# A written order from the output projection's last group to the MLP's third pair, with its norm by token halves

## The chip, the cores and the metric

The kernel runs on one core of one Trainium2 chip. The metric is device time in microseconds (us) of one execution, lower is better. Three runs of the kernel before took 2401.02, 2407.87 and 2409.24 us; their median, 2407.87, is the time before.

The core has five instruction streams that run beside each other and meet only at semaphores: PE (TensorE, matmuls; its weight loads are listed as PEld), DVE (VectorE), ACT (ScalarE), POOL (GpSimd) and SP (SyncE, which here only issues DMA transfers). Each stream works strictly in the order in which its instructions stand.

## The reference

One layer over 512 latent tokens of width 2048, with 256 context tokens as a prefix. All values are float32. The lines that matter here:

```python
mod_x = (silu(c) @ w_ada + b_ada)            # six rows of 2048: sh1, s1, g1, sh2, s2, g2
h  = rmsnorm(x, norm1_w) * (1 + s1) + sh1
q_da, k_da, v_da, q_mla, k_mla, v_mla = mixer_inputs(h, ...)   # projections of h, of the context too
o  = concat(differential attention, latent attention)          # 512 x 2048
x  = x + g1 * (o @ w_o)                                         # output projection
h2 = rmsnorm(x, norm2_w) * (1 + s2) + sh2                       # mean over the 2048 features of a token
g, u = split(h2 @ w_up)                                         # 2 x 5632
x  = x + g2 * ((silu(conv3(g)) * u) @ w_down)                   # conv3: over three neighbouring tokens
```

A final norm over `x` gives the output. `w_ada` is 2048 by 12288, so the modulation alone reads 96 MB.

## The kernel before

**Layout and precision.** Activations stand with features on the 128 partitions and the 512 tokens along the free axis, so a 2048-wide activation is 16 tiles of 128x512. Each float32 operand of a product is split into a high part (a rounded copy, made by ACT, `wh` for weights) and a low part (the remainder, made by DVE, `wl`), and a product is three matmuls: high·high, high·low, low·high (`mm3`, L107 to L109). Tiles are named after the buffers that they come from: `wr` raw weights of 128x1024, `a2k`, `q2k` and `b2k` activation tiles, `ada` a modulation row's weights, `xr` a tile of the residual `x`, `b` and `s` accumulators in PSUM.

**Weight blocks.** A block is 512 KB. SP issues its load into one of three raw buffers (`wraw`, L89), ACT makes the high part, DVE the low part, in one of three buffers each (`wblock`; L80 and L81 in the automatic order, L210 and L213 in the early written one, L1346 and L1352 in the late one).

**Modulation rows.** `gemv` (L171, L174) computes 128 of the 12288 modulation values: one 1 MB load into one of two `ada` buffers, then one multiply-and-sum on DVE over 128x2048. 64 of them are strewn over the program by `next_gemv`, one at a time, where the author of the order put them. In the early stages they are loaded by POOL's queue, in the output projection by SP's.

**The stages around the change.** First, the value stage: eight blocks of `w_v` go into six accumulators (`v0`), DVE and ACT write them away as high and low parts (`put_value`, the function `lay`), and the blocks of the next features follow. This region's order is written out: `step` puts a block's matmuls, then the high and low part of the block two further, then a list of small tasks; these tasks are the numbers of `plan` (L750) and the arguments at L790 and L791. In it nothing reorders.

Second, the output projection: the 16 output tiles are made in four groups of four; a group is eight blocks of `w_o`, 192 matmuls, 512 tokens wide. DVE then adds each accumulator to the residual (L1119), POOL's queue writes the result to `x1_d`, and ACT squares it; POOL adds the squares up over groups 0 to 2. The last four squares go straight into PE. `token_norm` (L1085) sums over features by a matmul with ones, L1093, ten passes at full width, and `rstd` (L162 to L167) makes the inverse root on ACT and DVE with one refinement step.

Third, the first pair of the MLP (`first_pair`): eight blocks of `w_up`, 384 products of 128x128 by 128x256 (the tokens in two halves), into four accumulators. Before a block, `normed` (L1155 to L1160) makes its two normed tiles, with high and low parts of each token half; `sums` (L1173 to L1181) makes from tiles j and j+8 the four sums of token halves and features that a Strassen-like scheme uses as moving operands in all later pairs. Between them stand the four "u" blocks (a third, classical, pair). Pair 3 is the first of that scheme (`run`, kind "p", L1376 and L1378). Its weights come through two rings of three raw buffers on SP's queue: ring a (`wr`) and ring b (`rb`, `Ring`, L1259).

From the output projection to the end of the first pair an automatic scheduler sets the order: it lists instructions per engine by its own estimate of when each can run. From the u blocks on the order is written out again (`tc.manual_schedule`): each engine's instructions stand as the Python code emits them.

## Time and profile before

| What | Before |
|---|---|
| median of 3 runs | 2407.87 us |
| profiled execution, its own time | 2408.41 us |
| its span, first to last instruction | 2406.6 us |
| PE busy | 2337.9 us (97%) |
| DVE busy | 1774.7 us (74%) |
| ACT busy | 1100.5 us (46%) |
| mean granted clock of TensorE | 0.992 |
| first matmul of output groups 0 to 3 | 835, 878.26, 921.80, 965.30 us |
| last group's end, first matmul of pair 3 | 1008.80, 1099.4 us |

The page gives for each engine its busy time, and for each group of instructions (by source line, engine, operation and tile) the number, busy time, mean duration and the idle time before them with what ended it. "L174 DVE ... ada<-ada" is read as: line 174 of the kernel, VectorE, writes `ada` from `ada`. A value in brackets with an arrow, such as "[2.40 <-DMA ada<-in_ada]", says how long the engine had waited before that instruction, and for what. "Granted clock" is the share of TensorE's full clock that it was given.

### The profile page before, as it was taken

To read this page: it belongs to the slowest core of one execution; us is meant where nothing else is said; L and a number is where in the kernel's file an instruction comes from. 1 tells how busy PE (TensorE), PEld (TensorE's weight loads), DVE (VectorE), ACT (ScalarE), POOL (GpSimd) and SP (SyncE) were. 2 spreads that over 40 slices of the span, in tenths; PEclk is the share of its full clock that TensorE was granted. 3 is DMA by queue.
4 is the path that set the end of the run, shared out by engine and by line. 5 is a ranking of instruction groups with operands and counts; after the bars stand their busy time and mean duration, and the time that the engine had idled before them with its cause. 6 is when DMAs were issued, how large, how long until landed. Compare 5 with 4: busy or idle time off the path is not lost.

```text
span 2406.6 us, 32350 instructions
## 1 busy us (share of the span) xinstructions
PE 2337.9 (97%) x12444; PEld 1967.4 (82%) x12444; DVE 1774.7 (74%) x2303; ACT 1100.5 (46%) x1660; POOL 271.2 (11%) x324
## 2 busy tenths in 40 slices
PE   8999999999999999999999999999999999999997
PEld 5787888777677788798888888888888888888887
DVE  5996787698878877597585757575767676766767
ACT  5322332455555622354454545454545454544553
POOL 0001001121100011200101010101010101111113
PEclk9999999999999999999999999999999999999999
DMA  9767877844311189514646454555554545455572
GB/s 381 280 224 273 307 286 291 246 138 121 119 42 49 61 317 346 186 59 135 143 130 144 128 143 136 140 140 140 134 147 126 150 120 157 123 157 123 140 213 78
DMA packets 141514, 407.45 MB, mean 169 GB/s; under 512 B 14880, under 2 KB 31792, under 8 KB 130736
## 3 DMA queue, kind: packets, MB, share of 16 engines
q1 hardware_dynamic: 107296, 298.42, 37.0%
q0 software_dynamic: 32912, 105.93, 18.2%
q8 instruction: 97, 1.59, 0.3%
q10 hardware_dynamic: 1152, 1.05, 0.1%
q14 instruction: 57, 0.47, 0.1%
HBM read 335.86 MB, written 69.48 MB: 168 GB/s over the span
## 4 chain that ended last, share of the span: by engine, by line
PE 69%; issue 14%; DVE 8%; ACT 3%; DMA 3%; POOL 2%; SPq 0%; POOLq 0%; DVEq 0%; ACTq 0%
PE y L1376 11%; PE b L107 7%; PE b L108 7%; PE b L109 7%; PE z L1376 6%; PE y L1378 5%; PE s L882 3%; PE z L1378 3%; PE x L1376 2%; PE s L108 2%; PE s L107 2%; PE s L109 2%; PE pt L894 1%; PE f L107 1%; PE x L1378 1%
## 5 line engine op out<-in xcount | busy, mean ns | idle before, releaser
L1397 POOL DMA_DIRECT2D x_d<-xs x160 | 140.6, 1018 | 1167.3 <-ACT xs L1396 1148.4
L107 PE MATMUL b<-ah,wh 128*128 128x512 f32 (+1 forms) x672 | 259.1, 386 | 0.0
L108 PE MATMUL b<-al,wh 128*128 128x512 f32 (+1 forms) x672 | 259.0, 385 | 0.0
L109 PE MATMUL b<-ah,wl 128*128 128x512 f32 (+1 forms) x672 | 258.0, 384 | 0.0
L1352 DVE TENSOR_TENSOR wl<-wr,wh 128x1024 fp32r<-128x1024 f32 x126 | 153.8, 1221 | 130.3 <-ACT wh L1346 130.2
L1352 DVE TENSOR_TENSOR wl<-rb,wh 128x1024 fp32r<-128x1024 f32 x124 | 151.1, 1220 | 127.5 <-ACT wh L1346 127.5
L1346 ACT CAST wh<-wr 128x1024 fp32r<-128x1024 f32 x126 | 132.3, 1050 | 206.9 <-PE b L108 100.5
L1346 ACT CAST wh<-rb 128x1024 fp32r<-128x1024 f32 x124 | 130.2, 1051 | 187.8 <-PE b L108 116.1
L1352 DVE TENSOR_TENSOR wl<-ws,wh 128x1024 fp32r<-128x1024 f32 x123 | 150.1, 1220 | 89.3 <-ACT wh L1346 89.3
L174 DVE CUSTOM_DVE_ANT_0 ada<-ada,cb,smt 128x2048 f32<-128x2048 f32 x64 | 153.5, 2401 | 58.5 <-DMA ada<-in_ada 58.5
L1346 ACT CAST wh<-ws 128x1024 fp32r<-128x1024 f32 x123 | 128.2, 1042 | 139.3 <-PE b L108 45.5
L109 PEld LDWEIGHTS b<-ah,wl 128*128 128x128 f32 x672 | 126.3, 188 | 25.6
L107 PEld LDWEIGHTS b<-ah,wh 128*128 128x128 f32 x672 | 126.6, 188 | 22.8
L108 PEld LDWEIGHTS b<-al,wh 128*128 128x128 f32 x672 | 126.6, 188 | 22.0
L107 PE MATMUL b<-a2k,wh 128*128 128x512 f32 (+1 forms) x352 | 135.2, 386 | 6.7 <-ACT a2k L1159 5.1
L109 PE MATMUL b<-a2k,wl 128*128 128x512 f32 (+1 forms) x352 | 133.2, 378 | 3.3 <-DVE wl L213 3.3
L80 ACT CAST wh<-wr 128x1024 fp32r<-128x1024 f32 (+2 forms) x64 | 64.2, 1003 | 135.3 <-PE s L108 44.3
L81 DVE TENSOR_TENSOR wl<-wr,wh 128x1024 fp32r<-128x1024 f32 (+2 forms) x64 | 77.8, 1215 | 42.5 <-ACT wh L80 42.3
L1376 PE MATMUL y<-b2k,wh 128*128 128x512 f32 x410 | 106.9, 391 | 0.0
L884 DVE TENSOR_REDUCE m<-s 128x1 f32<-128x768 f32 x96 | 90.1, 948 | 20.8 <-PE s L882 20.4
L1396 ACT ACTIVATE xs<-b,modx 128x512 f32<-128x512 f32 x160 | 101.1, 681 | 2.0 <-DMA x_d<-xs 1.6
L210 ACT CAST wh<-wr 128x1024 fp32r<-128x1024 f32 x38 | 39.9, 1050 | 126.7 <-DMA wr<-in_w_f 40.3
(536 smaller groups left out, 6095.7 us busy)
## 6 DMA issues: line engine op xcount, KB each, us to landing
rb<-in_w_up SPq DMA_DIRECT2D x123, 512.0 KB, 4.4
ada<-in_ada POOLq DMA_DIRECT2D x54, 1024.0 KB, 6.2
wr<-in_w_dn SPq DMA_DIRECT2D x84, 512.0 KB, 3.8
x_d<-xs POOLq DMA_DIRECT2D x160, 256.0 KB, 6.1
wr<-in_w_up SPq DMA_DIRECT2D x53, 512.0 KB, 4.2
ada<-in_ada SPq DMA_DIRECT2D x26, 1024.0 KB, 6.6
wr<-in_w_f SPq DMA_DIRECT2D x34, 512.0 KB, 6.2
adak<-in_ada_k SPq DMA_DIRECT2D x64, 256.0 KB, 5.4
```

The source lines that it names most:

```text
L81: ve.tensor_tensor(dst_l, src, dst_h.bitcast(F32), op=ALU.subtract)
L107: pe.matmul(out, st[0], mv[0], start=start, stop=False, **kw)
L108: pe.matmul(out, st[0], mv[1], start=False, stop=False, **kw)
L109: pe.matmul(out, st[1], mv[0], start=False, stop=stop, **kw)
L174: ve.tensor_tensor_reduce(out=junk, in0=w, in1=vec, op0=ALU.mult, op1=ALU.add, scale=1.0, scalar=col("b_ada", j), accum_out=dst[:, j:j + 1])
L884: ve.tensor_reduce(out=m, in_=s[:, :TT], axis=AX.X, op=ALU.max, negate=True)
L1346: sc.copy(hi, raw)
L1352: ve.tensor_tensor(lo, raw, hi.bitcast(F32), op=ALU.subtract)
L1376: pe.matmul(o, w[j][0], hs[j], start=start and j == 0, stop=False, skip_group_check=True)
L1378: pe.matmul(o[:, h0], w[j][1], hs[j][:, h0], start=False, stop=j == 7, skip_group_check=True)
L1396: sc.mul(x, po, modx[:, 80 + dt:81 + dt])
L1397: gp.dma_start(x1_d[dt], x, accum_op=ALU.add)
```

## The change

The change has two parts. One is small and early: in the value stage, the writing away of values 0 and 5 (`lay`) is put one step earlier, into the last value block's tasks, in the place of a modulation row, and the two steps behind it have three modulation rows where they had four, so that this place holds two rows fewer. Those two are made in the output projection instead, where every group now has a row ahead of its eighth block too.

The other part takes the stretch from the output projection's last group to the u blocks out of the automatic scheduler's hands and writes its order out for all five engines. In that order:

- weight blocks come by `load8`, `cast8`, `low8`: the load of block i+3 is issued by SP when DVE has made the low part of block i, and stands in SP's order directly behind it; a modulation row (`next_gemv`) stands behind each low part of the last output group;
- output blocks 6 and 7 run first for the first token half, then for the second; the sums of squares, the matmuls with ones, the root and the normed tiles are made by token halves, and the first two `w_up` blocks run by halves as well (`unit`);
- the normed tiles are held in tiles of the pools that the Strassen operands use (`tp`, `q2k(0)`), the sums are cut in two (`first` makes differences and high parts, `second` the low parts) and dealt out from a list by `some`;
- ring a's first loads follow from the same list of blocks; ring b's first loads are issued behind the third u block, where before both rings were filled at once;
- the convolution and activation of the first two feature tiles stand ahead of the u blocks, in PSUM tiles of the earlier pools.

The number of products, of modulation rows and of bytes loaded stays the same.

The diff, cut to its core (of the written region the added lines only):

```diff
+        def lay(t, own=False):
+            return lambda: put_value(0, v0, t, [rtmp(F32R), rtmp(F32R)] if own else None)
...
-                [gemvs(1), gemvs(1)], [gemvs(1), bias_out, gemvs(1)])
+                [gemvs(1), gemvs(1)], [gemvs(1), bias_out, lay(0), lay(5)])
...
-        step(block(1, 0), lay(0), lay(5), gemvs(1), lay(1, True), gemvs(1))
-        step(block(1, 1), lay(2), lay(3), gemvs(1), lay(4, True), gemvs(1))
+        step(block(1, 0), lay(1, True), gemvs(1), lay(2), gemvs(1))
+        step(block(1, 1), lay(3), gemvs(1), lay(4, True))
...
+    aq_ = [tc.alloc_tile_pool(name=f"aq{i}", bufs=8, side="right", reuse_waits="tile") for i in range(2)]
+
+    def q2k(i, dt=F32):
+        return aq_[i].tile([P, 512], dt, tag="q2k", name=nm("q2k"))
...
+    def square_tile():
+        return wx.tile([P, T], F32, tag="sq", name=nm("sq"), bufs=2)
+
+    def residual(dt):
+        xr = wx.tile([P, T], F32, tag="xr", name=nm("xr"), bufs=6)
+        nc.sync.dma_start(xr, x_t[dt])
+        return xr
+
+    def evict(dt, out, xr, c=slice(0, T)):
+        ve.scalar_tensor_tensor(out=x1[dt][:, c], in0=out[:, c], scalar=modx[:, 32 + dt:33 + dt], in1=xr[:, c],
+                                op0=ALU.mult, op1=ALU.add)
+
+    def out_block(outs, kb, w, c=slice(0, T), skip=True):
+        order = [(j, i) for j in range(2) for i in range(4)]
+        for j, i in sorted(order, key=lambda t: t[1]) if kb == 7 else order:
+            kt, o = kb * 2 + j, j * 512 + i * P
+            mm3(outs[i][:, c], [t[:, o:o + P] for t in w], [t[:, c] for t in osp[kt]], kt == 0, kt == 15, skip)
+
+    h0, h1 = slice(0, HT), slice(HT, T)
+    UP = [kb for j in range(4) for kb in (j, j + 4)]
+    src8 = [w_o[3, kb] for kb in range(8)] + [w_up0[kb] for kb in UP] + [w_up[0, 0, i] for i in range(2)]
+    raw8, hl8 = {}, {}
+
+    def load8(i):
+        if i < len(src8):
+            raw8[i] = wraw(src8[i])
+
+    def cast8(i):
+        hl8[i] = [wp.tile([P, 1024], F32R, tag=g, name=nm(g), bufs=3) for g in ("wh", "wl")]
+        sc.copy(hl8[i][0], raw8[i])
+
+    def low8(i):
+        ve.tensor_tensor(hl8[i][1], raw8.pop(i), hl8[i][0].bitcast(F32), op=ALU.subtract)
+        load8(i + 3)
+
+    x1, ss = [], wx.tile([P, T], F32, name="ss")
+    for g in range(3):
...
-            if kb != 7 if g else kb > 2:
+            if g or kb > 2:
                 next_gemv(wo, 1)
-            wh, wl = wblock(w_o[g, kb])
-            order = [(j, i) for j in range(2) for i in range(4)]
-            for j, i in sorted(order, key=lambda t: t[1]) if kb == 7 else order:
-                kt, o = kb * 2 + j, j * 512 + i * P
-                mm3(outs[i], (wh[:, o:o + P], wl[:, o:o + P]), osp[kt], kt == 0, kt == 15)
+            out_block(outs, kb, wblock(w_o[g, kb]), skip=False)
+        if g == 2:
+            for i in range(2):
+                hl8[i] = wblock(src8[i])
...
-        h = hf[kt] = hp.tile([P, T], F32, tag="h", name=nm("h"), bufs=5)
-        ve.scalar_tensor_tensor(out=h, in0=x1[kt], scalar=a2[:, kt:kt + 1], in1=r, op0=ALU.mult, op1=ALU.mult)
-        hx[kt] = (a2k(F32R), q2k(F32R) if kt >= 8 else hp.tile([P, T], F32R, tag="h12", name=nm("h12"), bufs=8))
...
+    def norm_in(kt, cs):
+        if ht[kt] is None:
+            ht[kt] = tp2k() if kt >= 8 else q2k(0)
+            hx[kt] = a2k(F32R), q2k(1, F32R) if kt >= 8 else hp.tile([P, T], F32R, tag="h12", name=nm("h12"), bufs=8)
+        c = slice(cs[0].start, cs[-1].stop)
+        ve.scalar_tensor_tensor(out=hview(kt, c), in0=x1[kt][:, c], scalar=a2[:, kt:kt + 1], in1=r[:, c],
+                                op0=ALU.mult, op1=ALU.mult)
+        for c in cs:
+            sc.activation(hx[kt][c is h1][:, h0], hview(kt, c), AF.Identity, bias=modx[:, 48 + kt:49 + kt])
+
+    def norm_low(kt, cs):
+        for c in cs:
+            hh, hl = half(hx[kt][c is h1])
+            ve.scalar_tensor_tensor(out=hl, in0=hview(kt, c), scalar=modx[:, 48 + kt:49 + kt], in1=hh.bitcast(F32),
+                                    op0=ALU.add, op1=ALU.subtract)
+
+    def normed(kts, *cs):
+        for kt in kts:
+            norm_in(kt, cs)
+        for kt in kts:
+            norm_low(kt, cs)
+
+    def scratch():
+        return hp.tile([P, T], F32, tag="d", name=nm("d"), bufs=2)
...
+        def first():
...
+            t1[j], t3[j], t2[j], t4[j] = q2k(0, F32R), tp2k(F32R), b2k(F32R), b2k(F32R)
+            for t, d in zip((t1, t2, t3, t4), ds):
+                sc.copy(half(t[j])[0], d)
...
+        def second():
+            for t, d in zip((t1, t2, t3, t4), ds):
+                hh, hl = half(t[j])
+                ve.tensor_tensor(hl, d, hh.bitcast(F32), op=ALU.subtract)
...
+    with tc.manual_schedule(engines=every):
+        for i in range(2, 5):
+            load8(i)
+        outs = [b_tile() for _ in range(4)]
+        xrs = []
+        for i in range(6):
+            out_block(outs, i, hl8.pop(i))
+            cast8(i + 2)
+            low8(i + 2)
+            next_gemv(wo, 2 if i == 2 else 1)
+            if i == 3:
+                xrs = [residual(12 + k) for k in range(4)]
+        wo.release()
+        hp = tc.alloc_tile_pool(name="hp", bufs=1, side="right", reuse_waits="tile")
+        r = hp.tile([P, T], F32, name="nr")
+        hp.tile([P, T], F32R, tag="h12", name=nm("h12"), bufs=8)
+        x1 += [b2k() for _ in range(4)]
+        for kb in (6, 7):
+            out_block(outs, kb, hl8[kb], h0)
+        s0, s1 = s_tile(), s_tile()
+        po = s0[:, :512]
+        fo = [s0[:, 512:], s1[:, :512], s1[:, 512:]]
+        sq = {}
+
+        def squares_of(c):
+            sq[c.start] = [t[:, k * HT:(k + 1) * HT] for t in (square_tile(), square_tile()) for k in range(2)]
+            for i in range(4):
+                evict(12 + i, outs[i], xrs[i], c)
+                sc.square(sq[c.start][i], x1[12 + i][:, c])
+
+        def ones_of(c):
+            qs = [ss[:, c]] + sq[c.start]
+            for q in qs:
+                pe.matmul(po[:, c], ones32, q, start=q is qs[0] and c is h0, stop=q is qs[-1], skip_group_check=True)
+
+        def root_of(c):
+            rstd(r[:, c], po[:, c], D, *half(scratch()))
+
+        def unit(n_, cs):
+            w = hl8[8 + n_]
             for j in range(2):
+                kt = UP[n_] * 2 + j
                 for i in range(4):
                     o = j * 512 + i * P
+                    classical(fo[i], kt, [t[:, o:o + P] for t in w], n_ == 0 and j == 0, n_ == 7 and j == 1, cs)
+
+        def pair(n_):
+            return [UP[n_] * 2 + j for j in range(2)]
+
+        cast8(8)
+        low8(8)
+        squares_of(h0)
+        out_block(outs, 6, hl8[6], h1)
+        ones_of(h0)
+        out_block(outs, 7, hl8[7], h1)
+        root_of(h0)
+        normed(pair(0), h0)
+        squares_of(h1)
+        for i in range(4):
+            gp.dma_start(x1_d[12 + i], x1[12 + i])
+        fo.append(b_tile())
+        unit(0, (h0,))
+        ones_of(h1)
+        cast8(9)
+        low8(9)
+        normed(pair(1), h0)
+        unit(1, (h0,))
+        cast8(10)
+        low8(10)
+        root_of(h1)
+        normed(pair(0), h1)
+        unit(0, (h1,))
+        normed(pair(1), h1)
+        cast8(11)
+        low8(11)
+        unit(1, (h1,))
+        normed(pair(2), h0, h1)
+        wx.release()
+        ff = tc.alloc_tile_pool(name="ff", bufs=1, reuse_waits="tile")
+        for n_ in range(2, 8):
+            unit(n_, (h0, h1))
+            cast8(10 + n_)
+            if n_ < 7:
+                normed(pair(n_ + 1), h0, h1)
+            low8(10 + n_)
+            some((0, 1, 2, 1, 2, 3)[n_ - 2])
...
-            items_a.append((job, w_up[0, job[1] // 2, job[1] % 2], 1))
+            if job[1] > 1:
+                items_a.append((job, w_up[0, job[1] // 2, job[1] % 2], 1))
...
-        ra, rb = Ring(wrp, "wr", 3, items_a), Ring(mm, "rb", 3, items_b)
+        ra = Ring(wrp, "wr", 3, items_a)
+        ra.pump()
...
-        cast(0)
-        low(0)
-        cast(1)
-        low(1)
+        for i in range(2):
+            ready[i] = *hl8.pop(16 + i), None, None
+        cast(2)
+        low(2)
+        for i in range(2):
+            t = convolve(i, fo[2 * i])
+            if i:
+                some(1)
+            acts[i] = multiply(silu(t), fo[2 * i + 1])
+            some(1 - i)
+            finish(t, acts[i])
+        ps_b.release()
+        ps_s.release()
...
+            if i == 2:
+                hp.release()
+                mm = tc.alloc_tile_pool(name="mm", bufs=1, side="right", reuse_waits="tile")
+                rb = Ring(mm, "rb", 3, items_b)
+                rb.pump()
...
-            cast(i + 2)
             if i:
+                cast(i + 2)
+            if i > 2:
                 act_after(i - 1)
                 vec_after(i - 1)
-            low(i + 2)
+            if i:
+                low(i + 2)
+            if i < 4:
+                some((2, 1, 0, 2)[i])
```

SP's order in the last output group, before from that group's fourth `w_o` block on, with the change from its sixth (`ada` a modulation row's load, `wr` a weight block's, the buffer numbers run on through the program). Before:

```order
L171 DMA ada_8700<-in_ada 128x2048
L89 DMA wr_8670<-in_w_o 128x1024
L171 DMA ada_8733<-in_ada 128x2048
L1117 DMA xr_8556<-in_x_t 128x512
L89 DMA wr_8703<-in_w_o 128x1024
L171 DMA ada_8766<-in_ada 128x2048
L89 DMA wr_8736<-in_w_o 128x1024
L89 DMA wr_8769<-in_w_o 128x1024
```

With the change:

```order
L89 DMA wr_8640<-in_w_o 128x1024
L171 DMA ada_8642<-in_ada 128x2048
L89 DMA wr_8673<-in_w_o 128x1024
L171 DMA ada_8675<-in_ada 128x2048
L89 DMA wr_8706<-in_w_o 128x1024
L171 DMA ada_8708<-in_ada 128x2048
L171 DMA ada_8711<-in_ada 128x2048
L89 DMA wr_8742<-in_w_up 128x1024
L171 DMA ada_8744<-in_ada 128x2048
```

Before, the loads of rows stood ahead of those of the weight blocks and the last of them ahead of the group's sixth block; now each row's load stands behind a weight block's load, down to those of `w_up`.

DVE's order at the same place (`wl` a low part, the two "ISA" rows of L174 one modulation row). Before, from the first low part of the group on:

```order
L81 TENSOR_TENSOR wl_8574<-wr_8571,wh_8573 128x1024
L174 ISA ada_8667,modx<-ada_8667,cb_7618,smt 128x2048
L174 ISA modx 128x1
L81 TENSOR_TENSOR wl_8607<-wr_8604,wh_8606 128x1024
L1119 SCALAR_TENSOR_TENSOR b2k_8534<-s_8269,modx,xr_8532 128x512
```

With the change, from its third low part on:

```order
L1114 TENSOR_TENSOR wl_8637<-wr_8602,wh_8636 128x1024
L174 ISA ada_8642,modx<-ada_8642,cb_7618,smt 128x2048
L174 ISA modx 128x1
L1114 TENSOR_TENSOR wl_8670<-wr_8604,wh_8669 128x1024
L174 ISA ada_8675,modx<-ada_8675,cb_7618,smt 128x2048
L1114 TENSOR_TENSOR wl_8703<-wr_8606,wh_8702 128x1024
L174 ISA ada_8708,modx<-ada_8708,cb_7618,smt 128x2048
L174 ISA ada_8711,modx<-ada_8711,cb_7618,smt 128x2048
L1114 TENSOR_TENSOR wl_8739<-wr_8640,wh_8738 128x1024
```

`wl_8670` stands behind the row whose load is `ada_8642`; SP's load `wr_8673` goes into the raw buffer that `wl_8670` reads, and the next row's load, `ada_8675`, stands behind it.

DVE's order behind the value stage (`beta` the copies at L735, `kl` and `rt` low parts of values). Before:

```order
L735 COPY beta<-b_1433 128x4
L174 ISA ada_2027,modx<-ada_2027,cb,smt 128x2048
L174 ISA modx 128x1
L81 TENSOR_TENSOR kl_2084<-b_1562,kh_2083 128x512
L213 TENSOR_TENSOR wl_2081<-wr_1959,wh_2080 128x1024
L81 TENSOR_TENSOR kl_2093<-b_1563,kh_2092 128x512
```

With the change:

```order
L735 COPY beta<-b_1433 128x4
L81 TENSOR_TENSOR kl_2028<-b_1562,kh_2027 128x512
L81 TENSOR_TENSOR kl_2034<-b_1563,kh_2033 128x512
L81 TENSOR_TENSOR rt_2093<-s_1560,rt_2092 128x512
L213 TENSOR_TENSOR wl_2090<-wr_1959,wh_2089 128x1024
L174 ISA ada_2101,modx<-ada_2101,cb,smt 128x2048
```

The row behind the copies is gone, and the two values that were written away behind and around the next low part stand ahead of it.

138 lines of the change are left out of this document (44 added, 94 removed).

## The prediction

> **What bounds the kernel now.** First the page's busy table, then the windows of the stretch that the change rewrites, from the last output group's first matmul (965.30) to the third MLP pair's first (1099.4).
>
> ```profile
> PE 2337.9 (97%) x12444; PEld 1967.4 (82%) x12444; DVE 1774.7 (74%) x2303; ACT 1100.5 (46%) x1660; POOL 271.2 (11%) x324
> ```
>
> ```profile
> 965.30:1008.80 43.50, 43.50 (x193) 36.05 (x192) 23.09 (x20) 10.71 (x13) 12.24 (x11) 1.00 0.58 203
> 1008.80:1019.25 10.45, 4.75 (x11) 1.63 (x10) 5.97 (x9) 5.11 (x9) 0.99 (x2) 0.96 0.45 172
> 1019.25:1086.00 66.75, 66.37 (x528) 66.14 (x528) 60.19 (x127) 38.00 (x78) 0.00 (x0) 0.95 0.20 66
> 1086.00:1099.40 13.40, 9.12 (x51) 8.64 (x51) 5.86 (x5) 3.07 (x4) 0.00 (x0) 0.75 0.51 184
> ```
>
> Columns are the stretch, its length, busy PE, PEld, DVE, ACT and POOL, the granted clock, the DMA share and GB/s. PE sets the pace and is full in the last output group; it idles 5.7 us around the norm and 4.3 us before pair 3, where the clock is 0.75 as well. The waits of PE name the two holes:
>
> ```profile
> PE b L107 <- ACT a2k L1159: 5.1, 1, 5.1
> PE z L107 <- ACT wh L1346: 3.6, 1, 3.6
> ```
>
> The first is the norm's chain, the second a w_up block whose load stood on SP behind three rb loads. With the slow clocks behind them the stretch, 134.1 us long, holds some 16 us that a better order could save. In the last output group DVE is half idle (23.09 of 43.50): all seven modulation rows (gemv, L174) of it are done at 979.9, because their loads ran ahead.
>
> **The first hunk (lay).** In the first value stage two modulation rows leave, and DVE reaches the splits sooner. One PE wait hangs on this:
>
> ```profile
> 257.99 2.35 DVE L174 CUSTOM_DVE_ANT_0 ada<-ada,cb,smt 128x2048 f32<-128x2048 f32 x1 [2.40 <-DMA ada<-in_ada]
> 260.27 1.22 DVE L213 TENSOR_TENSOR wl<-wr,wh 128x1024 fp32r<-128x1024 f32 x1
> 272.41 1.22 DVE L213 TENSOR_TENSOR wl<-wr,wh 128x1024 fp32r<-128x1024 f32 x1
> ```
>
> ```profile
> 273.69 0.50 PE L109 MATMUL b<-a2k,wl 128*128 128x512 f32 x1 [3.30 <-DVE wl L213]
> ```
>
> ```profile
> 270.00:274.00 4.00, 0.70 (x3) 0.30 (x2) 4.00 (x5) 1.16 (x2) 0.53 (x1) 1.00 0.59 131
> 274.00:280.00 6.00, 6.00 (x28) 5.13 (x26) 5.96 (x11) 0.67 (x2) 0.53 (x1) 0.72 0.87 355
> ```
>
> The split that PE wants at 270.4 ends at 273.6 since DVE waited for two modulation loads before 260. Without two of them (2.3 us each, and their waits) DVE comes at least 5 us sooner. That saves 3.30 us and, of the clock of 0.72 behind it, about 1.1 us (the twelve matmuls from 274.4 take 3.2 us instead of 2.1). Term: −4.4; bounds 0 (another wait takes it) and −4.9.
>
> **The last output group.** Its order is now written out, and here the change costs. In the new order SP issues a block's weight load only when DVE has made the low part three blocks earlier (the buffer is then free), and the modulation row's load stands behind it on SP. DVE makes the next low part only after that modulation row. So the load of row n+1 can't start before row n has landed and been reduced: DVE, SP and the DMA engines work in turn, six times. Before, the row's load stood ahead of its weight load and needed only the row before last. The prices of one round:
>
> ```profile
> 937.52 2.35 DVE L174 CUSTOM_DVE_ANT_0 ada<-ada,cb,smt 128x2048 f32<-128x2048 f32 x1 [0.34 <-DMA ada<-in_ada]
> 939.80 0.08 DVE L174 DVE_READ_ACCUMULATOR2_ANT modx<- 128x1 f32 x1
> 939.80 1.22 DVE L81 TENSOR_TENSOR wl<-wr,wh 128x1024 fp32r<-128x1024 f32 x1
> 1038.06 1.22 DVE L81 TENSOR_TENSOR wl<-wr,wh 128x1024 fp32r<-128x1024 f32 x1
> 1039.20 0.75 DVE L1155 SCALAR_TENSOR_TENSOR h<-b2k,a,nr 128x512 f32<-128x512 f32 x1
> ```
>
> ```profile
> DMA to landing us min/median/max: 4.6/6.5/9.8
> ```
>
> ```profile
> wr<-in_w_o SPq DMA_DIRECT2D x1, 512.0 KB, 3.5
> ```
>
> ```profile
> 949.75 0.33 SPq L171 DMA_DIRECT2D ada<-in_ada  x1
> ```
>
> The reduction takes 2.28 us from start to the next operation, the low part 1.14, two issues on SP about 0.42. The 1 MB load lands after 4.6 us at least (the fastest of all 64 issues of L171), 6.5 in the median, with the DMA engines some 95% busy. In the new order they are nearly idle, but 512 KB is issued 0.4 us ahead of the row. From 3.5 us for 512 KB and 4.6 for 1 MB, another 512 KB costs 1.1 us, so 1.5 MB ends near 5.7–5.9 after the first issue, 5.3–5.5 after the second. I take 5.5, nearer the lower end as the queue is short; bounds 4.6 and 6.5. A round is 0.42 + 5.5 + 2.28 + 1.14 = 9.3 us, against 5.44 us of PE per block (43.50/8).
>
> The Trainium skill ("DMA: Bandwidth & Descriptors", "Anatomy of one DMA — SWDGE (gpsimd) path") puts a transfer at about 2.0 us plus its bytes over 436 GB/s. By that 1 MB takes 4.4 us (the trace's fastest: 4.6) and the row here lands 5.2 us after its issue; the sum would be an estimated 1.8 us lower.
>
> Up to the end of the low part of w_up's first block, which the first evictions stand behind on DVE: start 3.3 us (cast 1.05, low 1.14, hand-offs, and about 1 us for the sums of squares on POOL, beside which a reduction took 3.51 and a low part 2.30); six rounds, 56.0; the second row in one round, 2.6 (its load lands after the first's, then 2.28). Sum 61.9.
>
> ```profile
> 971.93 3.51 DVE L174 CUSTOM_DVE_ANT_0 ada<-ada,cb,smt 128x2048 f32<-128x2048 f32 x1
> 975.38 2.30 DVE L81 TENSOR_TENSOR wl<-wr,wh 128x1024 fp32r<-128x1024 f32 x1
> ```
>
> PE would be at the end of its first halves after 38.3 us (six blocks of 5.44, two halves of 2.8). So PE starves, first at block 5 (due 27.2 us in; its low part comes after about 3.3 + 3·9.3 + 2.6 = 34 us), and the term is 61.9 − 38.3 = 23.6 us.
>
> **From there to pair 3.** All PE work that is left: 24·2 matmuls of the group's second halves, 96 of the first two blocks by halves, 288 of the other six, 192 of the u blocks, all 256 wide.
>
> ```profile
> 1030.00:1040.00 10.00, 10.00 (x85) 10.00 (x85) 10.00 (x24) 5.54 (x12) 0.00 (x0) 1.00 0.15 54
> ```
>
> ```profile
> 1010.42 3.71 PE b L1093 x8
> ...
> 1014.16 0.70 ACT nr L162
> 1014.88 0.64 ACT nr L163
> 1015.54 0.70 DVE n L165
> 1016.26 0.70 DVE n L166
> 1017.07 0.70 DVE nr L167
> 1017.90 0.76 DVE h L1155
> 1018.69 0.52 ACT a2k L1159
> ...
> 1031.24 0.40 DVE a2k L1160
> ```
>
> 85 in 10 us is 0.118 each (0.12 in the u blocks), so 73.8 us; the ten passes with ones, 0.46 each at full width, 4.6 in all. Halving a 512-wide matmul costs little (0.235 for 0.227). Then the waits. The norm's chain takes 5.1 us on full rows from the sum to PE; on halves, with DVE steps of 0.40 for 0.70 and ACT's a little shorter, 3.5. It lies beside the second halves of block 7 (2.8): 0.9 with the low part. Block 1's first half waits 1.2 (squares, then cast, low part and norm of its pair behind them on ACT and DVE), the second half's root 2.6 (a cast and a low part stand ahead of it), block 2 waits 1.1 for its pair. The first eviction costs 0.5, since the order lets the second half of a PSUM tile wait for it; PE restarts slow, 1.6. From block 2 on PE needs 5.64 us per block and DVE 0.66·2 + 4·0.40 + 1.14 for norm and low part, plus 2.9 per sum: even, as before, and covered. The rb loads now come after the u blocks' third, and pair 3 waits for a sum of them 0.8; the hidden part is under u block 3 (5.7), else they would cost 4.4. Waits 8.7; bounds 4 and 13. Sum 73.8 + 4.6 + 8.7 = 87.1.
>
> Whole stretch 61.9 + 87.1 = 149.0 for 134.1: **+14.9**. With −4.4: +10.5. The span 2406.6 becomes 2417.1, the profiled execution 2408.41 becomes 2418.9; the median of the runs is 0.5 lower, so I predict **2418.5**.
>
> Starved waits slow PE only when long: after the 3.30 us above the clock fell, after 2.20 us it did not (next matmul 0.39):
>
> ```profile
> 439.17 0.48 PE L882 MATMUL s<-ks,qs 128*128 128x512 f32 x1 [2.20 <-DVE kl L81]
> 439.48 0.39 PE L882 MATMUL s<-klz,qs 128*128 128x512 f32 x1
> ```
>
> **The rivals.** (1) *Faster.* The loads keep up, and the group stays PE's. Then its part is 38.3, the rest 87.1 less 2.1 for the restart: 123.3, −10.8, with the first hunk −15.2, 2392.7. For it speaks DVE's idle half of that group today; against it that a round must fit 5.44 us, so a load must land in 1.6 us, and the fastest is 4.6. Parity with today's time needs 3.7. Chance 8%, for a misread order.
> (2) *No change.* Loads land in 4.6: six times 0.9 less, 2413, or the later waits stay near 4 us. The fastest rows speak for it, the 512 KB ahead against. 25%.
> (3) *First hunk gains nothing*, since DVE meets value writes on the queue or the next wait (2.20 at 439) grows: 2423. 12%.
> (4) *Loads at today's median*, as evictions' writes and x rows share the queue: six times 1.0 more, 2424.5. 15%.
> The forecast itself 40%.
>
> **How the numbers follow.** A difference under 0.3% (7.2 us) can't be told from none. Slower: forecast, (3) and (4), 0.67; same (2400.6 to 2415.1): (2), 0.25; faster: (1), 0.08. Range: from (2) with 4 us fewer later waits, 2409, to (4) with half the first hunk's gain lost and two more us of waits, 2428.5; outside are (1) and a tenth more.
>
> **What would show it.** In the last output group DVE should idle before L174 for the ada DMA, 5 us each time, with L174 starting every 9 to 10 us instead of running ahead, and PE should wait for wl in its blocks 5 to 7, some 20 us in sum. The 5.1 us wait at the norm and the 3.6 before pair 3 should be gone, and so the 3.30 at 273. The forecast is wrong if L174 starts every 5 to 6 us there, or if the stretch from the group's first matmul to pair 3's is under 140 us.

## The result

The changed kernel takes 2443.07 us (median of 4 runs, 2440.42 to 2445.85) against 2406.15 us before: a ratio of 1.015, with a 95% interval of 1.0135 to 1.0165, so it is 1.5% slower. The prediction had the direction and missed the size: it said 2418.5 us, in a range that ended at 2428.5. The profiled execution (2440.42 us, span 2438.6) is 32.0 us longer than that of before (span 2406.6).

Where the 32.0 us lie, by the first matmuls of the stages on PE:

| stretch | before | after | difference | predicted |
|---|---|---|---|---|
| start to the last output group's first matmul | 965.3 | 959.4 | -5.9 | -4.4 |
| from there to the third pair's first matmul | 134.0 | 172.0 | +38.0 | +14.9 |
| from there to the end | 1307.3 | 1307.2 | -0.1 | 0 |

Before, the third pair's first matmul stands at 1099.25 us in the trace; the 1099.4 and 134.1 used ahead of the result are 0.15 too large.

The five largest waits of PE from 840 to 1160 us in the changed kernel (in all, how often, the longest):

```profile
PE b L109 <- DVE wl L1114: 16.4, 4, 7.7
PE y L107 <- DVE t L1312: 14.0, 1, 14.0
PE b L107 <- DVE b2k L1091: 5.2, 1, 5.2
PE s L107 <- ACT h L1165: 2.4, 1, 2.4
PE s L107 <- ACT a2k L1165: 1.6, 3, 0.6
```

The first and the third are the starvation that was forecast: 21.6 us in the last output group. The second, 14.0 us at the first u block, was not forecast at all. The norm's wait of 5.1 us and that of 3.6 before the third pair are gone, as they should be; the halves of the norm left four short waits, 4.0 us together.

The same stretch in windows of the changed kernel (columns as in the prediction: busy PE, PEld, DVE, ACT, POOL, granted clock, DMA share, GB/s). The cuts are the group's first matmul, PE's restart on the second token halves, the end of the first pair, the first u block, and the third pair:

```profile
959.36:1026.93 67.57, 45.91 (x193) 37.72 (x192) 26.91 (x25) 8.61 (x9) 6.22 (x7) 0.84 0.49 186
1026.93:1092.30 65.37, 60.88 (x452) 58.40 (x452) 50.71 (x101) 31.75 (x66) 2.16 (x4) 0.96 0.28 89
1092.30:1106.31 14.01, 0.01 (x1) 0.04 (x1) 10.82 (x24) 7.54 (x14) 0.00 (x0) 0.67 0.25 76
1106.31:1111.00 4.69, 4.69 (x23) 4.69 (x24) 2.44 (x6) 2.48 (x6) 0.00 (x0) 0.52 0.01 3
1111.00:1131.38 20.38, 20.38 (x172) 20.38 (x171) 12.59 (x26) 5.71 (x11) 0.00 (x0) 1.00 0.37 129
```

In the first window DVE is busy for 26.9 of 67.6 us and the DMA engines half the time, yet PE starves: nothing is full, each waits for the others in turn. The timeline of SP's queue and of DVE there shows the loop as the prediction drew it, a weight load, a row's load, and then the row's multiply-and-sum:

```profile
963.08 0.51 SPq L171 DMA_DIRECT2D ada<-in_ada  x1
974.54 0.33 SPq L89 DMA_DIRECT2D wr<-in_w_o  x1
974.92 0.42 SPq L171 DMA_DIRECT2D ada<-in_ada  x1
984.04 0.33 SPq L89 DMA_DIRECT2D wr<-in_w_o  x1
984.41 0.90 SPq L171 DMA_DIRECT2D ada<-in_ada  x2
...
1006.17 0.43 SPq L171 DMA_DIRECT2D ada<-in_ada  x1
```

```profile
971.01 2.35 DVE L174 CUSTOM_DVE_ANT_0 ada<-ada,cb,smt 128x2048 f32<-128x2048 f32 x1 [8.34 <-DMA ada<-in_ada]
980.51 2.35 DVE L174 CUSTOM_DVE_ANT_0 ada<-ada,cb,smt 128x2048 f32<-128x2048 f32 x1 [6.00 <-DMA ada<-in_ada]
982.79 1.22 DVE L1114 TENSOR_TENSOR wl<-wr,wh 128x1024 fp32r<-128x1024 f32 x1
990.28 2.35 DVE L174 CUSTOM_DVE_ANT_0 ada<-ada,cb,smt 128x2048 f32<-128x2048 f32 x1 [6.27 <-DMA ada<-in_ada]
...
1013.08 2.35 DVE L174 CUSTOM_DVE_ANT_0 ada<-ada,cb,smt 128x2048 f32<-128x2048 f32 x1 [7.31 <-DMA ada<-in_ada]
```

The row issued at 974.92 is used at 980.51, the low part behind it ends at 984.0, and the next weight load is issued at 984.04: a round of 9.5 us. The whole stretch of 14.0 us at the u blocks is one chain between DVE and ACT. The timeline of these two:

```profile
1096.35 0.74 DVE L1310 SCALAR_TENSOR_TENSOR t<-s,smt,t 128x511 f32<-128x511 f32 x1
1098.13 0.75 DVE L1312 SCALAR_TENSOR_TENSOR t<-s,smt,t 128x511 f32<-128x511 f32 x1
1101.15 0.69 DVE L1321 TENSOR_TENSOR t<-t,s 128x512 f32<-128x512 f32 x1 [2.27 <-ACT t L1317]
1103.10 0.68 DVE L1327 TENSOR_TENSOR al<-t,ah 128x512 fp32r<-128x512 f32 x1
1105.41 0.75 DVE L1312 SCALAR_TENSOR_TENSOR t<-s,smt,t 128x511 f32<-128x511 f32 x1
```

```profile
1099.19 1.28 ACT L1317 ACT_TABLE_LOAD   x1
1100.49 0.63 ACT L1317 ACTIVATE t<-t 128x512 f32<-128x512 f32 x1
1103.82 0.78 ACT L1305 ACTIVATE t<-s,smt 128x512 f32<-128x512 f32 x1 [1.33 <-DVE al L1327]
```

The convolution of the first feature tile, its activation, its product and its split run to the end before the second one may begin, because both use the one tile `t`, and differences and low parts of the Strassen sums stand between the steps. The u blocks' first accumulator lies in the PSUM banks of the first pair's accumulators, so PE waits until the second convolution has read them, at 1106.2.

### The profile page after: what moved, and what is told of

It is laid out like the page before. It is cut to its first block, busy times and chain, and to the rows that moved or that the text cites. A ratio compares the mean times of both kernels' runs of the same rounds, so it can differ in the third digit from the quotient of the medians.

```text
span 2438.6 us, 32460 instructions
## 1 busy us (share of the span) xinstructions
PE 2343.6 (96%) x12502; PEld 1974.4 (81%) x12502; DVE 1778.1 (73%) x2315; ACT 1101.5 (45%) x1666; POOL 268.0 (11%) x322
## 4 chain that ended last, share of the span: by engine, by line
PE 73%; issue 10%; DVE 8%; DMA 4%; ACT 3%; POOL 2%; SPq 0%; DVEq 0%; POOLq 0%; ACTq 0%
PE y L1467 12%; PE b L107 8%; PE b L108 8%; PE b L109 7%; PE z L1467 6%; PE y L1469 6%; PE z L1469 3%; PE s L883 3%; PE s L108 2%; PE x L1467 2%; PE s L109 2%; PE s L107 2%; DMA ada<-in_ada 2%; PE x L1469 1%; PE pt L895 1%
## 5 line engine op out<-in xcount | busy, mean ns | idle before, releaser
L174 DVE CUSTOM_DVE_ANT_0 ada<-ada,cb,smt 128x2048 f32<-128x2048 f32 x64 | 153.8, 2406 | 96.4 <-DMA ada<-in_ada 96.3
L109 PEld LDWEIGHTS b<-ah,wl 128*128 128x128 f32 x672 | 126.3, 188 | 25.6
L80 ACT CAST wh<-wr 128x1024 fp32r<-128x1024 f32 (+2 forms) x50 | 49.6, 992 | 109.4 <-DMA wr<-in_w_o 61.3
L107 PE MATMUL s<-a2k,wh 128*128 128x512 f32 (+1 forms) x240 | 89.9, 375 | 1.6 <-ACT a2k L1165 1.6
L109 PEld LDWEIGHTS b<-a2k,wl 128*128 128x128 f32 x336 | 66.8, 199 | 30.0 <-DVE wl L1114 17.7
```

The costliest lines, as they stand in the source:

```text
L107: pe.matmul(out, st[0], mv[0], start=start, stop=False, **kw)
L109: pe.matmul(out, st[1], mv[0], start=False, stop=stop, **kw)
L174: ve.tensor_tensor_reduce(out=junk, in0=w, in1=vec, op0=ALU.mult, op1=ALU.add, scale=1.0, scalar=col("b_ada", j), accum_out=dst[:, j:j + 1])
```

## The experiments

All ratios are to the kernel before, which was run beside each kernel (medians 2404.81 to 2407.12 us), with 95% intervals. They are those of the repeated runs as recorded, and not quotients of the medians in the table. "Stretch" is taken from the profiled executions, from the last output group's first matmul to the start of the third pair's last product (seventh of seven), since a loss can hide inside that pair. It is split at the third pair's first matmul:

| kernel | to the third pair | in it | stretch | time, us | ratio |
|---|---|---|---|---|---|
| before | 134.0 | 16.9 | 150.9 | 2405 to 2407 | 1 |
| the change | 172.0 | 18.0 | 190.0 | 2443.07 | 1.0150 (1.0135 to 1.0165) |
| u accumulators in free banks | 165.6 | 25.8 | 191.4 | 2442.46 | 1.0149 (1.0125 to 1.0173) |
| no rows in the last group | 142.1 | 18.0 | 160.0 | 2413.83 | 1.0027 (1.0013 to 1.0040) |
| rows loaded ahead | 141.6 | 18.0 | 159.6 | 2411.58 | 1.0018 (1.0007 to 1.0029) |
| rows ahead and free banks | 135.5 | 25.5 | 161.0 | 2414.76 | 1.0032 (1.0019 to 1.0044) |
| the same, convolutions side by side | 125.5 | 25.3 | 150.8 | 2403.54 | 0.9985 (0.9973 to 0.9996) |
| the same, low parts on POOL | 125.7 | 25.6 | 151.3 | 2406.07 | 0.9996 (0.9981 to 1.0012) |
| side by side, last sums later | 125.7 | 24.6 | 150.3 | 2403.88 | 0.9987 (0.9974 to 1.0001) |
| before, first part of the change alone | 131.6 | 16.9 | 148.5 | 2399.53 | 0.9983 (0.9967 to 0.9998) |
| the same, ring b's loads later | 126.5 | 16.9 | 143.4 | 2397.96 | 0.9956 (0.9942 to 0.9970) |

### The loop in the last output group

Two runs ask whether the rows make the loop, and whether it is the rows as such or their place in SP's order. The first leaves the seven rows of that group out, and with them a part of the modulation:

```diff
-            next_gemv(wo, 2 if i == 2 else 1)
+            for _ in range(2 if i == 2 else 1):
+                j = next(gv, None)
+                if j is not None:
+                    ve.memset(modx[:, j:j + 1], 0.0)
```

> The changed kernel without the seven modulation rows in the last output group: no load, no multiply-and-sum, their values set to zero instead, so that part of the modulation is left out. Theory A (serial loop of row load, multiply-and-sum, low part and next load): without rows the group's first halves end at PE's own pace, 38.3 us after its first matmul instead of 67, and PE waits there fall from 21.6 us to under 3: about 2443 - 28 = 2415. Theory B (the written order of the weight loads alone, three raw buffers, starves PE): PE waits of 10 us or more stay, 2430 or more.

The second keeps all rows and DVE's order, and moves each row's load one place ahead of the weight load that waits for DVE (`row_in` issues the next row's load on SP, `row_sum` is the multiply-and-sum of a row that is on its way):

```diff
     def low8(i):
         ve.tensor_tensor(hl8[i][1], raw8.pop(i), hl8[i][0].bitcast(F32), op=ALU.subtract)
+        if i < 8 and len(came) < 7:
+            row_in()
         load8(i + 3)
...
+        row_in()
         for i in range(2, 5):
             load8(i)
...
-            next_gemv(wo, 2 if i == 2 else 1)
+            row_sum(i + (i > 2))
+            if i == 2:
+                row_in()
+                row_sum(3)
```

> The changed kernel with all rows, but in SP's order each row's load one place earlier, ahead of the weight load that waits for DVE's low part; the first stands ahead of the group's first weight loads. DVE's order stays. Theory A (the order on SP makes the loop): two rows are under way at a time, a row is there when DVE wants it, and the group comes within 4 us of the run without rows: 2443 - 25 = 2418, L174's successor line starting every 5 to 6 us. Theory B (the 7 MB of rows need their time on the DMA engines and DVE whatever the order): less than 10 us gained, 2433 or more.

Without rows the time falls by 29 us, to 2413.83; with all rows loaded one place earlier it falls by 31 us, to 2411.58. The two stretches are the same within 0.4 us, so the rows cost nothing once their loads no longer wait for DVE. In the run with the loads ahead, the group's window and the rows' sums on DVE read:

```profile
961.37:1004.61 43.24, 43.24 (x228) 37.40 (x226) 30.34 (x27) 10.30 (x13) 7.70 (x7) 1.00 0.75 278
```

```profile
975.43 2.35 DVE L1131 CUSTOM_DVE_ANT_0 ada<-ada,cb,smt 128x2048 f32<-128x2048 f32 x1 [0.90 <-DMA ada<-in_ada]
...
994.12 2.35 DVE L1131 CUSTOM_DVE_ANT_0 ada<-ada,cb,smt 128x2048 f32<-128x2048 f32 x1 [2.23 <-DMA ada<-in_ada]
```

PE is full for all of the group, at full clock, and DVE waits 0.9 to 2.2 us for a row where it waits at all, not 6 to 8. The same bytes, the same DVE work and the same DVE order: what made the loop was one place in SP's order. Theory B of both runs (weight loads or the rows' own time as the limit) falls.

### The wait at the u blocks

Two runs move both u accumulators into banks that are free (the second accumulator `z` twice, instead of `y` and `z`), one from the changed kernel and one from the run with rows ahead:

```diff
-                    y = b_tile("y", 2)
+                    b_tile("y", 2)
                     b_tile()
-                    live["s"] = [y, b_tile("z", 2)]
+                    live["s"] = [b_tile("z", 2), b_tile("z", 2)]
```

> The changed kernel, with the four u blocks' two accumulators both in PSUM banks that nothing uses any more, instead of one of them in the banks of the first pair's accumulators; nothing else moves. Theory A (bank wait): the 14.0 us wait of PE at the first u block is only for the convolutions that still read those banks, so it goes, with the 2.2 us of half clock behind it: about 16 us less than the changed kernel, 2427, and no PE wait for t before the u blocks. Theory B (DVE bound): DVE has 25.8 us of work from there to the third pair, so the wait only moves to low parts or Strassen sums, and 5 us or less are gained: 2438 or more.

> Both edits: the rows' loads one place earlier and both u accumulators in free banks. If the two losses are independent the gains add up: 2443 - 25 - 16 = 2402, some 4 us under the kernel before. If DVE is the bound behind the first pair, 2412 or more.

The wait for `t` went, and the time did not change: 2442.46 against 2443.07, and 2414.76 against 2411.58. The timeline of PE in the first of them shows where the 14.0 us are now:

```profile
1116.23 0.58 PE L107 MATMUL z<-a2k,wh 128*128 128x256 f32 x1 [6.78 <-ACT wh L1435]
1117.49 0.58 PE L109 MATMUL z<-a2k,wl 128*128 128x256 f32 x1 [0.47 <-DVE wl L1441]
1137.22 2.08 PE L1467 MATMUL y<-b2k,wh 128*128 128x512 f32 x4 [6.34 <-ACT m L1389]
```

The third pair begins 6.5 us earlier and takes 7.9 us longer. PE waits for the fourth u block's high part, which stands on ACT behind both activation chains and two sums, and then for a copy on ACT in the third pair. So the bank wait was real and was not the limit: theory A falls. What ACT and DVE have to do there in written order was late behind it anyway.

The next run keeps both edits and changes that order. The two convolutions stand next to each other, the second one in a tile of its own. The sums that stood between them and ahead of the fourth u block's high part stand behind it, but for one half of a sum, which moves ahead, to the first pair's last block:

```diff
-            some((0, 1, 2, 1, 2, 3)[n_ - 2])
+            some((0, 1, 2, 1, 2, 4)[n_ - 2])
...
-    def gate_in(ft, g):
-        t = ff.tile([P, T], F32, tag="t", name=nm("t"), bufs=1)
+    def gate_in(ft, g, t=None):
+        t = t or ff.tile([P, T], F32, tag="t", name=nm("t"), bufs=1)
...
-        for i in range(2):
-            t = convolve(i, fo[2 * i])
-            if i:
-                some(1)
-            acts[i] = multiply(silu(t), fo[2 * i + 1])
-            some(1 - i)
-            finish(t, acts[i])
+        ts = [gate_in(i, fo[2 * i], scratch() if i else None) for i in range(2)]
+        for i in range(2):
+            silu(convolve(i, fo[2 * i], ts[i]))
+        for i in range(2):
+            acts[i] = multiply(ts[i], fo[2 * i + 1])
+        for i in range(2):
+            finish(ts[i], acts[i])
...
-                some((2, 1, 0, 2)[i])
+                some((0, 2, 2, 2)[i])
```

> The run with the rows' loads one place earlier and both u accumulators in free banks, with the order behind the first pair changed: the two convolutions stand next to each other on ACT and DVE, the second in a tile of its own, so that they no longer wait for each other, and the sums that stood between and behind them stand behind the third and fourth u blocks' high and low parts. Theory C (the written order of ACT and DVE behind the first pair is the bound; the bank wait only showed where): the 6.8 us wait for the fourth u block's high part and the 5.8 us wait in the third pair go, about 12 to 15 us less: 2400 to 2403, under the kernel before. Theory D (DVE's amount of work is the bound): the waits stay at 8 us or more in sum, 2410 or more.

The time falls by 11.2 us, from 2414.76 to 2403.54, to a ratio of 0.9985 of the kernel before. The wait for the fourth block's high part is gone; that in the third pair stayed. Windows of the u blocks and of 19.5 us from the third pair's first matmul, and PE's row:

```profile
1062.50:1085.55 23.05, 23.05 (x194) 23.05 (x193) 21.39 (x44) 14.23 (x27) 0.00 (x0) 1.00 0.40 139
1085.55:1105.00 19.45, 13.76 (x64) 11.71 (x63) 16.36 (x23) 8.71 (x14) 0.00 (x0) 0.82 0.26 78
```

```profile
1096.99 2.50 PE L1488 MATMUL y<-b2k,wh 128*128 128x512 f32 x5 [5.69 <-ACT m L1410]
```

PE runs through the u blocks, but DVE is now busy 21.4 of 23.1 us beside them. The time is the one that theory C expected, within 1 us, and not the 2410 or more of theory D. But of the two waits that C let go only one went; the other one, 5.7 us, stays. Two runs tried to tell what holds it. The first moves DVE work to POOL:

```diff
-                ve.tensor_tensor(hl, d, hh.bitcast(F32), op=ALU.subtract)
+                (gp if j > 3 and (t is t3 or t is t4) else ve).tensor_tensor(hl, d, hh.bitcast(F32), op=ALU.subtract)
```

> The run before this one (convolutions side by side, sums behind the u blocks) with eight of its 32 low parts of Strassen operands, those of the third and fourth sum of tiles 4 to 7, made by POOL instead of DVE: 2.7 us of DVE's work (8 times 0.34) move to an engine that is idle there and takes 0.80 us for such an operation. Theory D (behind the first pair DVE's amount of work is the bound: it is busy 21.4 of the 23.1 us of the u blocks): the 5.7 us wait of PE in the third pair falls by 2 us or more and the time by 2 to 4 us, 2400. Theory C (only the order of the written stream): the wait stays within 1 us. Rival to both: an operation of POOL slows DVE's beside it, as at the output groups (2.30 us for a low part instead of 1.22), and nothing is gained or some is lost.

The second puts the last tile's sums behind the weight sum of the third pair:

```diff
-            if i < 4:
-                some((0, 2, 2, 2)[i])
+            if i < 5:
+                some((0, 2, 2, 0, 2)[i])
```

> The run with the convolutions side by side and the sums behind the u blocks (all low parts on DVE again), with the last two sums' halves (tile 7's) put behind the weight sum and the low part of the third pair's third weight operand, where they stood ahead of them. Theory C (order: the weight sum that the third pair's third product needs, and with it the copy on ACT, stands behind the sums on DVE): DVE makes that weight sum 3.2 us earlier, and PE's 5.7 us wait falls to 3.5 or less, 2 to 3 us in time. Theory D (amount): the wait of PE moves to the operand b2k of the same product, in sum 5 us or more, and nothing is gained.

Neither gained: 2406.07 and 2403.88, with waits of 6.7 and 5.6 us at the same instruction. In the first, POOL took up to 1.84 us for an operation that was put at 0.80, and a low part of a weight block on DVE beside it 1.70 instead of 1.22, so the trace shows the third possibility of that expectation, each engine slower where the other works beside it; theory D stays untested by it. The lines of that run, first the operations of POOL at the new place (shortest, median, longest, ns), then DVE's group:

```profile
L1218 POOL TENSOR_TENSOR tp<-d,tp x4: 742/1498/1836, 1068.7 to 1090.6; 128x256 fp32r<-128x256 f32 x4
```

```profile
L1462 DVE TENSOR_TENSOR wl<-rb,wh 128x1024 fp32r<-128x1024 f32 x1 | 1.7, 1703 | 0.0
```

In the second, the weight sum did come 3 us earlier (1.5 us after the third pair's first matmul, not 4.6), and the copy that PE waits for no earlier, 10.7 us after that matmul instead of 10.8: it then stood on ACT behind the copies of the sums that had been moved. That run's two rows:

```profile
1098.91 0.41 ACT L1213 CAST q2k<-d 128x256 fp32r<-128x256 f32 x1 [1.69 <-DVE d L1209]
1101.09 0.57 ACT L1410 COPY m<-y 128x512 f32<-128x512 f32 x1
```

So this wait survived two further arrangements of the work. ACT's rows say which link is late: the copy stands in ACT's order behind the high part of a weight sum (`ws`) and an activation. These two ends of that chain, in the kernel before and in the run with the convolutions side by side:

```profile
1099.37 1.05 ACT L1346 CAST wh<-ws 128x1024 fp32r<-128x1024 f32 x1 [7.42 <-PE z L108]
...
1104.24 0.57 ACT L1300 COPY m<-y 128x512 f32<-128x512 f32 x1
```

```profile
1091.51 1.04 ACT L1456 CAST wh<-ws 128x1024 fp32r<-128x1024 f32 x1 [1.79 <-DVE ws L1429]
...
1096.37 0.58 ACT L1410 COPY m<-y 128x512 f32<-128x512 f32 x1
```

The chain takes 4.9 us in both. Before, it starts 0.1 us after the third pair's first matmul, here 6.0 us after it, since the weight sum stands on DVE behind the last Strassen sums. In the run with the last sums later it starts at 2.8 us, but the moved sums' copies stretch it to 7.9. An order with these copies behind the copy `m` was not run. Whether it would remove the wait, or DVE's amount of work forbids it, stays open.

### The early part, and the kernel before with one edit

The first part of the change alone, on the kernel before (its edits are those of the first three pieces of the diff, and a row ahead of every group's eighth block):

> The kernel before with the first part of the change alone: values 0 and 5 written away one step earlier, two modulation rows moved from the value stage to the output projection. Theory A (the prediction's term): 4.4 us less, 2402 or a ratio of 0.998, and no PE wait for wl at L213. Theory B (the value stage waits for transfers that vary from run to run; the last output group's first matmul stood at 961.4, 966.5 and 970.6 us in three kernels with the same early program): the waits move to the copies of beta, and the median stays within 2 us, ratio 0.999 to 1.001.

2399.53 us, a ratio of 0.9983 (0.9967 to 0.9998): 4.1 us less, with an interval of 0.5 to 7.9, while the medians of the two kernels, 2399.53 and 2407.12, differ by 7.6. The wait of 3.3 us for `wl` at L213 is gone in this run and in every other one with this edit. But the waits for the copies of beta at L735 moved between 0.2 and 5.4 us among these kernels, whose early program is the same, and the last output group's first matmul between 959.2 and 970.6. The 5.9 us that the two profiled executions show at that point are inside this scatter; the 4.1 us of the repeated runs are the better figure, and its interval nearly reaches zero.

Last, that kernel with one more edit, which the profile of before asked for: the w_up block that PE waited for stood on SP behind three loads of ring b. Here a ring no longer fills itself when it is made, and ring b's first loads are issued behind the low parts of the first two u blocks:

```diff
-        ra, rb = Ring(wrp, "wr", 3, items_a), Ring(mm, "rb", 3, items_b)
+        ra, rb = Ring(wrp, "wr", 3, items_a), Ring(mm, "rb", 3, items_b)
+        ra.pump()
...
         cast(1)
         low(1)
+        rb.pump()
```

> The run before this one, with one more edit: ring b's three first loads are issued behind ring a's for the fourth u block and the third pair instead of ahead of them on SP. Theory: the 3.6 us wait for the fourth u block's high part, 0.7 for its low part, and the half clock behind them (about 3 us) go: 7 us less than the run before this one, the third pair's first matmul some 7 us nearer to the last output group's first. Rival: the transfers of ring b, now later, make the third pair wait for its weight sums instead: 2 us or less gained.

The waits of PE in its late part:

```profile
PE b L107 <- ACT a2k L1159: 5.1, 1, 5.1
PE b L1093 <- ACT sq L1092: 0.6, 1, 0.6
PE b L108 <- DVE a2k L1160: 0.4, 1, 0.4
```

The waits ahead of the third pair are gone, nothing took their place, and the stretch is 143.4 us, 5.1 less than without the edit. That is less than the 7 us expected; the waits that the edit removes were 3.0 us in the profiled execution without it, and 4.3 in that of the kernel before. The whole time is less clear: the median falls by 1.6 us, the ratios lie 0.27% apart, which is 6.5 us, and their intervals just touch. At 0.9956 (0.9942 to 0.9970) this kernel is faster than the kernel before, and apart from the two edits it has the order of before.

## Why the prediction was right and wrong

**The bound and the loop: right, 5 us too small.** The prediction put the group, up to the end of the low part ahead of the first evictions, at 61.9 us; that low part ended 67.0 us after the group's first matmul, and PE restarted at 67.6. The round was put at 0.42 + 5.5 + 2.28 + 1.14 = 9.3 and the four measured rounds with one row are 9.5, 9.8, 10.8 and 9.9. Only the landing was too short: the six rows that were waited for took 7.9, 5.6, 5.9, 5.7, 6.9 and 6.0 us from issue to use, 6.3 in the mean, against the chosen 5.5; six times 0.8 is the missing 5 us. The choice "nearer the lower end as the queue is short" was wrong, and the DMA engines, taken to be nearly idle, were busy for 0.49 of that window; the median of before, 6.5, would have been nearer. The formula of the Trainium skill that was weighed there ("DMA: Bandwidth & Descriptors", "Anatomy of one DMA — SWDGE (gpsimd) path") gave an estimated 5.2 and was further off still: no row here was that fast. The page states that fit for transfers issued by GpSimd; these rows are issued by SP. The rows and their order were the cause, as the two runs with 29 and 31 us gained show.

**The step that failed: "From there to pair 3".** It was put at 87.1 us and took 104.5, counted from PE's restart. Its list of waits (8.7 us, bounds 4 and 13) went through norm, root, squares, loads of ring b. It held nothing for the start of the u blocks: it never asked where their accumulators lie and what still reads those banks, nor what ACT and DVE have to do there. It was there to be seen: in the written order the first matmul of the u blocks waits for DVE and ACT, while in the kernel before the accumulators `y` and `z` have banks of their own. The term put at nothing measured 14.0 us, and 2.3 us of half clock behind it (the window from 1106.31 to 1111.00 at 0.52). The rest of the step is off by only 1.1 us, and that is luck: the listed waits came to 4.0 us of 8.7, and the matmuls, slow stretches included, to 84.2 instead of 78.4.

**A wait is not a cause.** The correction "14 us for a bank" would have failed as well: with free banks the time stayed, and PE waited 6.8 and 6.3 us at two later places for the same work of ACT and DVE. The sentence "From block 2 on PE needs 5.64 us per block and DVE ... even, as before, and covered" holds for the blocks themselves, but it costs the sums at what the order places there: nine of sixteen half steps. The other seven were left for the activation chains and the u blocks, and the prediction had not priced DVE and ACT there. Before, DVE did these sums under the first pair and the first two u blocks (the first two windows below), where it was busy 39.26 of 40.70 us and 19.56 of 20.36; beside the other two u blocks it was idle for most of the time:

```profile
1019.25:1059.95 40.70, 40.70 (x316) 40.68 (x317) 39.26 (x83) 24.25 (x52) 0.00 (x0) 0.93 0.20 65
1059.95:1080.31 20.36, 19.98 (x166) 19.78 (x165) 19.56 (x43) 13.02 (x25) 0.00 (x0) 1.00 0.03 4
1080.31:1099.25 18.94, 14.66 (x98) 14.18 (x97) 7.24 (x7) 3.76 (x5) 0.00 (x0) 0.82 0.62 220
```

So before, the last sum was finished 19 us ahead of the third pair's first matmul. In the changed kernel it was finished just at that matmul, and in the run with the convolutions side by side 4.7 us behind it.

**The first hunk: right.** The term was -4.4; alone it measures -4.1, with an interval from -7.9 to -0.5, and the wait it named is gone. That it could be eaten by another wait (rival 3) happened in single executions and not in the median.

**The rivals.** Faster (1) needed a round within 5.44 us and fell with the first row. No change at 2413 (2) needed loads of 4.6 us, and none of them was that fast; its other condition, later waits near 4 us, held, and was not enough. Loads at the median (4) describes the loop better than the forecast does; with the u blocks' wait added, 2424.5 + 16.3 is 2440.8, close to the 2443.07 measured. No rival had that wait, so the range, built on bounds of terms that were on the list, ended at 2428.5.

**The halves of the norm gained little.** With the loop gone the norm's wait of 5.1 us is four short waits of 4.0, and with all three repairs the third pair begins 125.5 us after the group's first matmul instead of 134.0. Most of that is not due to the halves: the kernel before with the first part of the change and ring b's loads later, its norm at full width, comes to 126.5. And with all three repairs the third pair itself takes 25.3 us instead of 16.9, so that the stretch is as long as before (150.8 and 150.9): the gain is given back one stage later, at the copy on ACT that starts late because DVE is still at the sums. The 0.15% by which that kernel is under before is no more than the first hunk's.

## What to carry to other kernels

When an order is written out by hand, follow each queue round once: if a load stands behind a load that waits for an engine, and that engine waits for the first load's data, the three work in turn, however idle each looks; one place in the order cost 31 us here. A wait names the resource that was released last, not what is late: take the wait away, and compare the time up to a point well behind it, since 6.5 us gained at the third pair were lost within that pair. And price the work that a new order leaves for later, not only the work it places in the stretch that was looked at.

## What the hardware showed

Half clock does not follow from the length of a wait alone. In the changed kernel PE stood still for 2.33 us and the clock fell to 0.57 over the next 4 us; a hole of 2.38 us later left it at 1.00:

```profile
981.73:984.06 2.33, 0.00 (x0) 0.00 (x0) 2.28 (x3) 0.41 (x1) 0.00 (x0) 1.00 0.00 0
984.06:988.00 3.94, 3.94 (x10) 3.14 (x11) 0.00 (x0) 0.00 (x0) 0.00 (x0) 0.57 0.71 254
1047.65:1050.03 2.38, 0.01 (x1) 0.01 (x1) 2.10 (x6) 0.57 (x2) 0.00 (x0) 1.00 0.65 220
1050.03:1054.00 3.97, 3.83 (x29) 3.63 (x30) 2.54 (x6) 1.77 (x4) 0.00 (x0) 1.00 0.00 0
```

The same hole, at the same instruction, is in the seven other kernels with the written order, 2.37 to 2.39 us long, and in each of them the clock fell, to between 0.57 and 0.72 over the next 4 us. The run with the rows loaded ahead:

```profile
1018.01:1020.39 2.38, 0.01 (x1) 0.00 (x0) 2.10 (x6) 0.56 (x2) 0.00 (x0) 1.00 0.73 220
1020.39:1024.36 3.97, 3.83 (x17) 3.63 (x18) 2.55 (x6) 1.26 (x3) 0.00 (x0) 0.57 0.00 0
```

So the prediction's "only when long", read from one hole of 3.30 us and one of 2.20, does not hold at this length.

The Trainium skill ("TensorE: Matmul & The Clock Gate", "What's actually happening") says that activity is judged in windows of about 3.4 us that run freely, and that the clock is halved after at least one idle window. A free-running window fits opposite outcomes at the same length; but an idle time of 2.33 us is shorter than a whole such window and halved the clock all the same, so here the measurement differs from the page and decides. In the last output group these dips cost nothing of their own, since the loop, not PE, set the pace.

The early value stage varied more than expected: eight executions, one each of kernels with the same early program, reached the last output group between 959.2 and 970.6 us. A gain of a few us cannot be read from one pair of profiles behind such a stage.
